# Modulation steps moved into the mixers' query and key stages, and a reordered beginning

## The chip, the cores and the metric
The kernel runs on one core of a Trainium2 chip. The metric is the device time of one execution in microseconds. Three runs of the kernel before gave 1868.36, 1869.28 and 1870.40 us, median 1869.28. The profile is of one further execution.

## The reference, cut to what matters
One inference step of a hybrid diffusion transformer, two layers, 384 tokens of width 1024 in three tiles of 128 (tile 0 context, tiles 1 and 2 latent). All is float32.
```
m = silu(c) @ w_ada + b_ada            # per layer and condition: 9 rows of 1024
x = layernorm(ALPHA*x + 0.5*m[2]*swiglu(modulate(x, m[0], m[1])))      # FFN 1
h = modulate(x, m[3], m[4])
u = h @ w_in                           # fourier | q latent | kv latent | rope key | na q,k,v
y_m = attention(rmsnorm(u_q) @ w_uq, [c_kv @ w_ukv | rope key], v)     # 8 heads
x = layernorm(ALPHA*x + m[5]*((g_f*y_f + g_m*y_m + g_n*y_n) @ w_out))  # gates: sigmoid(h @ w_gate)
x = layernorm(ALPHA*x + 0.5*m[8]*swiglu(modulate(x, m[6], m[7])))      # FFN 2
modulate(x, shift, scale) = ln(x)*(1+scale) + shift
```

## The kernel before
Matrices are multiplied as three products of rounded halves: a weight or activation is split into a high part (`whi`, cast on ACT, line 188) and the remainder (`wlo`, subtraction on DVE, line 193), and PE multiplies hi*hi, hi*lo and lo*hi. Nearly all other instructions carry line 77, where a helper issues them, so names of tiles tell them apart.

PSUM is one pool of eight banks (`psum`, tag "b") handed out in rotation: a new tile takes the bank of the one eight tiles earlier and waits until that one has been read. SBUF slots rotate likewise. SP issues the weight loads at places found by a planner (`make_plan`, `place`); elsewhere each engine's order comes from the scheduler that compiles the program, near program order. `begin` alone is under a manual schedule: there PE, ACT and DVE run in the order of the code.

The modulation rows of later sublayers are computed in pieces beside the main work. `ada_step` loads 128x1024 of `w_ada` and multiplies it into two accumulators `acc` on DVE (one per condition; the first step of a block is a TENSOR_SCALAR, the others SCALAR_TENSOR_TENSOR). After eight steps `ada_finish` transposes (`at`) and reduces (`red`) both on DVE, and three calls later `ada_place` puts a PE product `ada<-red,quad` into a bank, from which DVE adds the bias into `mod`. `ada_spend(n)` does n steps, up to a budget for each sublayer: 12 for the mixer of layer 0, 8 for that of layer 1. In the mixer it is called in `value` (nv), after `load_bias(0)` and before each nq and nk group.

`mixer_body` goes in this order: turns of the q latents (`qnT`), Fourier mixing (`fa`, `fo`, `oF`), the kv latents (`ckT`), `query` for three tiles (`q`, `qtok`), the rope key (`krT`), keys (`kn`, four groups, split by DVE into `k`), values (`v`, four groups, split into `vs`), turned queries (`qT`, split into `q`), then the Fourier branch `yb` in eight groups, copied by DVE to `mg`, and the attention, which begins with `s`. The mixer's head (uq, kv, uf; `qn` is the rms-normed q latent, `f` the split Fourier input) precedes it.

`begin` handles the first sublayer: 24 identity transposes (`warm`), statistics of the three tiles on DVE, normalised tiles `xn`, their transposes `xT`, copies `hf`, then for each of eight chunks the first modulation (`ada_first`: 16 small products `ada`, a DVE transpose `adas`; `ada_first_finish`: `adat`, `mod`), the modulated halves `hmh` and `hml`, and the first products `hd` of the FFN.
Of the kernel before, what the change touches and what calls it, by code (L numbers as in the profile page):

```python
# [8 lines left out]
F32 = mybir.dt.float32  # L9
F32R = mybir.dt.float32r  # L10
AF = mybir.ActivationFunctionType
ALU = mybir.AluOpType
AX = mybir.AxisListType
# [3 lines left out]
P = 128  # L17
# [71 lines left out]
class Kernel:  # L89
# [279 lines left out]
    def ada_setup(self):  # L369
        self.ada_blocks = [("g", (0, 0)), ("m", (0, 1), 0), ("m", (0, 1), 1), ("g", (0, 1)), ("m", (0, 2), 0), ("m", (0, 2), 1),  # L370
                           ("g", (0, 2)), ("m", (1, 0), 0), ("m", (1, 0), 1), ("g", (1, 0)), ("m", (1, 1), 0), ("m", (1, 1), 1),
                           ("g", (1, 1)), ("m", (1, 2), 0), ("m", (1, 2), 1), ("g", (1, 2))]
        self.ada_pos, self.ada_fin, self.ada_due = 0, [], []
        self.mod = {}
        self.gate_d = {}
        sel = self.fixed([P, 32], F32, "sel")
        self.nc.vector.tensor_reduce(out=sel, in_=self.ident.rearrange("p (q r) -> p r q", q=4), op=ALU.add, axis=AX.X)
        self.quad = self.fixed([P, 4, 32], F32, "quad")
        self.nc.gpsimd.tensor_copy(out=self.quad, in_=sel.unsqueeze(1).broadcast_to([P, 4, 32]))
        self.bad = [self.fixed([P, 72], F32, "bad") for _ in range(DEPTH)]  # L380

    def ada_bias(self, l):
# [240 lines left out]
    def transition(self, prev, nxt, mod):  # L623
# [65 lines left out]
            p()  # L689
        self.inhead = False  # L690

    def begin(self, nxt):
        nc = self.nc
        hf = [self.slot([P, 2, TOK], F32, "hf") for _ in range(4)]
        ns, mvs, rs = [], [], []

        def normal(t):
            n = self.slot([P, D], F32, "xn")
            if t == NT - 1:
                nc.vector.tensor_scalar(out=n, in0=self.x[t], scalar1=mvs[t][:, 0:1], scalar2=rs[t], op0=ALU.subtract, op1=ALU.mult)  # L700
            else:
                mr = self.small(1)
                nc.vector.scalar_tensor_tensor(out=mr, in0=mvs[t][:, 0:1], scalar=-1.0, in1=rs[t], op0=ALU.mult, op1=ALU.mult)
                nc.scalar.activation(out=n, in_=self.x[t], func=AF.Identity, scale=rs[t], bias=mr)
            ns.append(n)

        for t in range(NT):
            mvs.append(self.stats(self.x[t]))
            rs.append(self.rstd(mvs[t][:, 1:2], 1.0, 1e-6))
            if t:  # L710
                normal(t - 1)

        def turn(t, then=None, qs=range(2)):
            for q in qs:
                pt = self.psum("xT")
                for b in range(4):
                    dc = q * 4 + b
                    nc.tensor.transpose(pt[:, b * P:(b + 1) * P], ns[t][:, dc * P:(dc + 1) * P], self.ident)
                if then and q == 0:
                    then()  # L720
                for b in range(2):
                    o, i = hf[2 * q + b][:, :, t * P:(t + 1) * P], pt[:, b * 256:b * 256 + 256].rearrange("p (a b) -> p a b", a=2)
                    if b:
                        nc.scalar.copy(out=o, in_=i)
                    else:
                        nc.vector.tensor_copy(out=o, in_=i)

        piece = {0: 1, 1: 1, 2: 1, 3: 1, 4: 2, 6: 2}
        m = self.mod_tile((0, 0))

        hg = {}

        def shift(dc, *cds):
            h = hf[dc // 2][:, dc % 2]
            if dc not in hg:
                hg[dc] = self.slot([P, TOK], F32, "hg")
            g = hg[dc]
            for cd in cds:
                c = (slice(0, P), slice(P, TOK))[cd]
                sc, sh = m[:, 1, dc, cd:cd + 1], m[:, 0, dc, cd:cd + 1]  # L740
                nc.scalar.activation(out=self.hm[0][:, dc, c], in_=h[:, c], func=AF.Identity, scale=sc, bias=sh)
                nc.vector.tensor_scalar(out=g[:, c], in0=h[:, c], scalar1=sc, scalar2=sh, op0=ALU.mult, op1=ALU.add)
            for cd in cds:
                c = (slice(0, P), slice(P, TOK))[cd]
                nc.vector.tensor_tensor(out=self.hm[1][:, dc, c], in0=g[:, c], in1=self.hm[0][:, dc, c].bitcast(F32), op=ALU.subtract)

        turn(0)
        self.ada_bias(0)
        normal(NT - 1)
        self.held = []  # L750
        ahead = self.ada_first(0, 1)
        nxt.cold_unit(0)
        turn(1, self.high)
        self.ada_first_finish(0, 1, ahead)
        shift(0, 0)
        turn(2, qs=[0])
        shift(0, 1)
        self.low()
        turn(2, qs=[1])
        every = [(t, g) for t in range(NT) for g in range(HG)]  # L760
        for dc in range(KD):
            d1 = dc + 1
            if d1 < KD:
                nxt.cold_unit(d1)
            if dc:
                parts, i, j = [(p, t, g) for t, g in every for p in range(3)], 6, 9
            else:
                parts, i, j = [(p, t, g) for ps, ts in (((0, 1), (0,)), ((0, 1), (1, 2)), ((2,), range(NT))) for p in ps for t in ts for g in range(HG)], 12, 15
            if not dc:
                self.high()  # L770
                self.low()
            nxt.cold_head(dc, parts[:i])
            self.high()
            self.low()
            if d1 in piece:
                ahead = self.ada_first(d1, piece[d1])
            nxt.cold_head(dc, parts[i:j])
            if d1 in piece:
                self.ada_first_finish(d1, piece[d1], ahead)
            if d1 < KD:  # L780
                shift(d1, 0, 1)
            nxt.cold_head(dc, parts[j:])
            while self.held:
                self.high()
                self.low()
        self.held = None
        nxt.cold_finish()
        self.ada_bias(1)
        self.gate_start()
# [179 lines left out]
    def mixer_body(self, ph):  # L969
        nc, I, K, O, l = self.nc, self.I, self.K, self.O, ph.l  # L970
# [60 lines left out]
            ckT.append(kt)  # L1031

        def query(t):
            c = slice(t * P, (t + 1) * P)
            qk = self.slot([P, NH, HQ], F32, "qtok")
            for hh in range(2):
                b = self.psum("q")
                for kc in range(3):
                    w = self.W(("wuq", l, kc), "mla_w_uq", l, kc * P, 1, 0, 768)
                    self.mm3(b[:, 0:384], (qnT[kc][:, 0, c], qnT[kc][:, 1, c]),  # L1040
                             tuple(x[:, 0, hh * 384:hh * 384 + 384] for x in w), kc == 0, kc == 2)
                bv = b[:, 0:384].rearrange("p (h j) -> p h j", h=4)
                qs = qk[:, 4 * hh:4 * hh + 4]
                if t == 0:
                    nc.scalar.copy(out=qs, in_=bv)
                else:
                    nc.scalar.copy(out=qs[:, :, 0:64], in_=bv[:, :, 0:64])
                    self.rope(qs[:, :, 64:96], bv[:, :, 64:96], t - 1, 4)
            qtok.append(qk)
# [6 lines left out]
        pt = self.psum("krT")  # L1056
# [4 lines left out]
        k96 = [self.slot([HQ, 2, 512], F32R, "k96") for _ in range(NH)]  # L1061
        w = self.ukv(l, 0)
        for pr in range(4):
            b = self.psum("kn")
            for kc in range(2):
                lhs = tuple(x[:, kc, 2 * pr:2 * pr + 2].rearrange("p a b -> p (a b)") for x in w)
                self.mm3(b, lhs, (ckT[kc][:, 0], ckT[kc][:, 1]), kc == 0, kc == 1)
            for e in range(2):
                kk = k96[2 * pr + e]
                self.split(kk[0:64, 0], kk[0:64, 1], b[64 * e:64 * e + 64, :])  # L1070
                nc.vector.tensor_copy(out=kk[64:96], in_=krt[64:96].bitcast(F32))
        w = self.ukv(l, 1)
        vm = []
        for t in range(4):
            b = self.psum("v")
            for kc in range(2):
                self.mm3(b, (ckT[kc][:, 0, t * P:(t + 1) * P], ckT[kc][:, 1, t * P:(t + 1) * P]),
                         tuple(x[:, kc].rearrange("p a b -> p (a b)") for x in w), kc == 0, kc == 1)
            vm.append(self.split_v(b))
# [21 lines left out]
        for d in range(KD):  # L1101
            b = self.branch_chunk(l, 0, d, oF)
# [51 lines left out]
        for p2 in range(4):  # L1154
            for nme in ("nq", "nk"):
                self.ada_spend(1)
                b = self.psum(nme)
# [107 lines left out]
    def run(self):  # L1265
# [7 lines left out]
        self.mhalf = self.fixed([P, 1], F32, "mhalf")  # L1273
        nc.vector.memset(self.mhalf, -0.5)

        wp = self.psum("warm")
        for i in range(24):
            nc.tensor.transpose(wp[:, i % 4 * P:i % 4 * P + P], self.ident, self.ident)
        self.mask = self.fixed([P, 64], F32, "mask")
        self.rp = self.fixed([P, 2, 2, 32], F32, "rp")  # L1280
        self.ada_setup()
# [292 lines left out]
```

## Time and profile before
| | |
|---|---|
| runs | 1868.36 to 1870.40 us, median 1869.28 |
| profiled execution | 1866.74 us, span 1865.0 us |
| PE busy | 99% of the span |
| DVE busy | 1409.0 us, 76% |
| ACT busy | 785.3 us, 42% |
| DMA | mean 172 GB/s |

The span runs from the first to the last instruction. The profile marks an engine busy while it executes; a PE wait of a few microseconds is a hundredth of the span or less and can be seen only in the waits and in rows in order of time.

### The profile page before, as it was taken

To read this page: it belongs to the slowest core of one execution; us is meant where nothing else is said; L and a number is where in the kernel's file an instruction comes from. 1 tells how busy PE (TensorE), PEld (TensorE's weight loads), DVE (VectorE), ACT (ScalarE), POOL (GpSimd) and SP (SyncE) were. 2 spreads that over 40 slices of the span, in tenths; PEclk is the share of its full clock that TensorE was granted. 3 is DMA by queue.
4 is the path that set the end of the run, shared out by engine and by line. 5 is a ranking of instruction groups with operands and counts; after the bars stand their busy time and mean duration, and the time that the engine had idled before them with its cause. 6 is when DMAs were issued, how large, how long until landed. Compare 5 with 4: busy or idle time off the path is not lost. (4 is left out here: it accounts for less than half of the span.)

```text
span 1865.0 us, 27258 instructions
## 1 busy us (share of the span) xinstructions
PE 1842.9 (99%) x10568; PEld 1728.1 (93%) x10568; DVE 1409.0 (76%) x2206; ACT 785.3 (42%) x1305; POOL 94.7 (5%) x115
## 2 busy tenths in 40 slices
PE   8999999999999999999999999999999999999998
PEld 6899998999899999999999999989999998999997
DVE  6788888689997677888876888978798776533345
ACT  4433335556355453332453333355554553533330
POOL 0000002000100010000000000120001000000000
PEclk9999999999999999999999999999999999999999
DMA  9766656234835446666545666542356353444522
GB/s 325 264 224 212 206 209 207 88 102 126 234 109 188 125 148 221 196 226 219 188 159 186 221 220 219 193 157 89 113 177 183 104 190 130 133 135 125 145 92 79
DMA packets 225602, 320.22 MB, mean 172 GB/s; under 512 B 32784, under 2 KB 181888, under 8 KB 225344
## 3 DMA queue, kind: packets, MB, share of 16 engines
q1 hardware_dynamic: 223328, 313.88, 52.5%
q0 software_dynamic: 2112, 4.59, 0.6%
q8 instruction: 83, 1.36, 0.3%
q14 instruction: 47, 0.39, 0.1%
q10 hardware_dynamic: 32, 0.01, 0.0%
HBM read 312.32 MB, written 8.02 MB: 172 GB/s over the span
## 5 line engine op out<-in xcount | busy, mean ns | idle before, releaser
L193 DVE TENSOR_TENSOR wlo<-raw,whi 128x1024 fp32r<-128x1024 f32 (+4 forms) x420 | 488.7, 1181 | 148.7 <-ACT whi L188 68.0
L188 ACT CAST whi<-raw 128x1024 fp32r<-128x1024 f32 (+4 forms) x420 | 420.3, 1020 | 325.9 <-DVE wlo L193 83.7
L77 PE MATMUL w<-hmh,whi 128*128 128x384 f32 x1152 | 388.3, 337 | 0.8 <-ACT sl L77 0.8
L77 PE MATMUL w<-hmh,wlo 128*128 128x384 f32 x1152 | 387.1, 336 | 0.0
L77 PE MATMUL w<-hml,whi 128*128 128x384 f32 x1152 | 387.1, 336 | 0.0
L77 PE MATMUL y<-whi,sT 128*128 128x512 f32 x1050 | 335.1, 391 | 1.7 <-DVE sT L77 1.5
L77 DVE SCALAR_TENSOR_TENSOR acc<-raw,cs,acc 128x1024 f32<-128x1024 f32 x236 | 296.9, 1290 | 28.8 <-DMA raw<-in_w_ada_dram 28.5
L77 PEld LDWEIGHTS y<-whi,sT 128*128 128x128 f32 x1050 | 196.8, 188 | 41.1 <-DVE sT L77 2.1
L77 PEld LDWEIGHTS w<-hmh,whi 128*128 128x128 f32 x1152 | 216.6, 188 | 3.2 <-ACT sl L77 1.1
L77 PEld LDWEIGHTS w<-hml,whi 128*128 128x128 f32 x1152 | 216.6, 188 | 1.9
L77 PEld LDWEIGHTS w<-hmh,wlo 128*128 128x128 f32 x1152 | 216.6, 188 | 0.0
L77 PE MATMUL y<-wlo,sT 128*128 128x512 f32 x525 | 204.2, 389 | 0.0
L77 PE MATMUL g<-hmh,whi 128*128 128x384 f32 x384 | 132.5, 345 | 1.4 <-DVE qN L77 1.4
L77 PE MATMUL g<-hmh,wlo 128*128 128x384 f32 x384 | 129.8, 338 | 1.6 <-DVE wlo L193 1.6
L77 PE MATMUL g<-hml,whi 128*128 128x384 f32 x384 | 129.9, 338 | 0.0
L77 PEld LDWEIGHTS y<-wlo,sT 128*128 128x128 f32 x525 | 98.6, 188 | 18.1
L77 ACT CAST sT<-sl 128x384 fp32r<-128x384 f32 x72 | 37.1, 515 | 183.8 <-DVE sl L77 183.8
L77 PE MATMUL hd<-whi,hmh 128*128 128x256 f32 (+1 forms) x336 | 100.1, 300 | 1.6 <-ACT hmh L77 1.6
L77 PE MATMUL hd<-wlo,hmh 128*128 128x256 f32 (+1 forms) x336 | 99.0, 297 | 0.0
L77 PE MATMUL hd<-whi,hml 128*128 128x256 f32 (+1 forms) x336 | 98.9, 296 | 0.0
L77 ACT ACTIVATE sl<-w 128x384 f32<-128x384 f32 x72 | 35.4, 492 | 110.0 <-PE w L77 109.7
L77 POOL TENSOR_TENSOR st<-st,mhalf 128x1 f32<-128x1 f32 x48 | 43.9, 916 | 689.3 <-DVE st L77 689.2
(271 smaller groups left out, 2952.3 us busy)
## 6 DMA issues: line engine op xcount, KB each, us to landing
raw<-in_ffn_w_dram SPq DMA_DIRECT2D x244, 512.0 KB, 5.0
raw<-in_w_ada_dram SPq DMA_DIRECT2D x128, 512.0 KB, 4.9
raw<-in_w_gate_dram SPq DMA_DIRECT2D x48, 512.0 KB, 4.1
raw<-in_w_in_dram SPq DMA_DIRECT2D x32, 512.0 KB, 6.1
raw<-in_w_ada_dram SPq DMA_DIRECT2D x32, 256.0 KB, 5.9
raw<-in_w_out_dram SPq DMA_DIRECT2D x16, 512.0 KB, 6.8
raw<-gd SPq DMA_DIRECT2D x12, 512.0 KB, 5.1
raw<-in_ffn_w_dram SPq DMA_DIRECT2D x22, 256.0 KB, 5.8
```

Of the source, the lines that this page charges most:

```text
L77: r = f(*a, **kw)
L188: self.real.scalar.copy(out=hi, in_=r)
L193: self.real.vector.tensor_tensor(out=lo, in0=r, in1=hi.bitcast(F32), op=ALU.subtract)
```

## The change
Six edits: (1) the `sel` reduction and the `quad` copy move from the setup to behind the statistics; (2) 14 more identity transposes at the start of `begin`; (3) the tile before is normalised between the two halves of a tile's statistics; (4) turns and copies are separate, and the hf copies of tiles 1 and 2 come behind the first modulation; (5) `ada_first` comes ahead of the weight split of its turn; (6) the mixer spends modulation steps in `query` (1 each), before each kn group (1) and before v groups 1 and 3 (1), from the same budgets.
```
     def ada_setup(self):
...
-        sel = self.fixed([P, 32], F32, "sel")
-        self.nc.vector.tensor_reduce(out=sel, in_=self.ident.rearrange("p (q r) -> p r q", q=4), op=ALU.add, axis=AX.X)
-        self.nc.gpsimd.tensor_copy(out=self.quad, in_=sel.unsqueeze(1).broadcast_to([P, 4, 32]))
+        self.sel = self.fixed([P, 32], F32, "sel")
...
+    def warm(self, n):
+        wp = self.psum("warm")
+        for i in range(n):
+            self.nc.tensor.transpose(wp[:, i % 4 * P:i % 4 * P + P], self.ident, self.ident)
...
     def begin(self, nxt):
+        self.warm(14)
...
         for t in range(NT):
-            mvs.append(self.stats(self.x[t]))
+            st = self.small(12)
+            for h in range(2):
+                nc.vector.bn_stats(out=st[:, h * 6:h * 6 + 6], in_=self.x[t][:, h * 512:h * 512 + 512])
+                if t and h == 0:
+                    normal(t - 1)
+            mvs.append(self.moments(st, 2))
             rs.append(self.rstd(mvs[t][:, 1:2], 1.0, 1e-6))
-            if t:
-                normal(t - 1)
+        nc.vector.tensor_reduce(out=self.sel, in_=self.ident.rearrange("p (q r) -> p r q", q=4), op=ALU.add, axis=AX.X)
+        nc.gpsimd.tensor_copy(out=self.quad, in_=self.sel.unsqueeze(1).broadcast_to([P, 4, 32]))
...
-        turn(0)
+        for q in range(2):
+            copy(*turn(0, q))
...
-        turn(1, self.high)
+        wait = [turn(1, 0), turn(1, 1)]
+        self.high()
         self.ada_first_finish(0, 1, ahead)
         shift(0, 0)
-        turn(2, qs=[0])
+        wait.insert(1, turn(2, 0))
+        for _ in range(2):
+            copy(*wait.pop(0))
         shift(0, 1)
         self.low()
-        turn(2, qs=[1])
+        wait.append(turn(2, 1))
+        for w in wait:
+            copy(*w)
...
+            if d1 in piece:
+                ahead = self.ada_first(d1, piece[d1])
             self.high()
             self.low()
-            if d1 in piece:
-                ahead = self.ada_first(d1, piece[d1])
...
         def query(t):
+            self.ada_spend(1)
...
         for pr in range(4):
+            self.ada_spend(1)
             b = self.psum("kn")
...
         for t in range(4):
+            self.ada_spend(t % 2)
             b = self.psum("v")
```
On DVE, layer 0, before: the splits of the second to fourth kn group (`k`), a weight split among them.
```order
L77 TENSOR_TENSOR k_650_3491<-kn_3512,k_650_3491 64x512
L77 CAST k_650_3491<-krt_3486 32x1024
L77 CAST k_651_3492<-krt_3486 32x1024
L77 TENSOR_TENSOR k_651_3492<-kn_3512,k_651_3492 64x512
L193 TENSOR_TENSOR wlo_3530<-raw_3261,whi_3529 128x1024
L77 TENSOR_TENSOR k_652_3493<-kn_3525,k_652_3493 64x512
L77 CAST k_652_3493<-krt_3486 32x1024
L77 CAST k_653_3494<-krt_3486 32x1024
L77 TENSOR_TENSOR k_653_3494<-kn_3525,k_653_3494 64x512
L77 TENSOR_TENSOR k_654_3495<-kn_3542,k_654_3495 64x512
```
After, the same place: steps of modulation stand among the groups.
```order
L77 STREAM_TRANSPOSE at_3546<-acc_2399 128x1024
L77 STREAM_TRANSPOSE at_3549<-acc_2400 128x1024
L77 TENSOR_REDUCE red_3545<-at_3546 128x32
L77 TENSOR_REDUCE red_3545<-at_3549 128x32
L77 TENSOR_SCALAR acc_3552<-raw_3307,cs_156 128x1024
L77 TENSOR_SCALAR acc_3553<-raw_3307,cs_156 128x1024
L77 TENSOR_TENSOR k_657_3524<-kn_3558,k_657_3524 64x512
L77 CAST k_657_3524<-krt_3519 32x1024
L77 CAST k_658_3525<-krt_3519 32x1024
L77 TENSOR_TENSOR k_658_3525<-kn_3558,k_658_3525 64x512
L77 SCALAR_TENSOR_TENSOR acc_3552<-raw_3327,cs_156,acc_3552 128x1024
L77 SCALAR_TENSOR_TENSOR acc_3553<-raw_3327,cs_156,acc_3553 128x1024
```
The transposes, reductions and products of the modulation have come in between the k splits.

On PE, layer 0, before: the end of kn and the beginning of v.
```order
L77 MATMUL kn_3542<-ckT_3338,wlo_3311 128x512
L77 MATMUL kn_3542<-ckT_3348,whi_3310 128x512 x2
L77 MATMUL kn_3542<-ckT_3348,wlo_3311 128x512
L77 MATMUL v_3555<-whi_3397,ckT_3338 128x512
L77 MATMUL v_3555<-wlo_3398,ckT_3338 128x512
```
After, the same place.
```order
L77 MATMUL kn_3594<-ckT_3375,whi_3337 128x512 x2
L77 MATMUL kn_3594<-ckT_3375,wlo_3338 128x512
L77 MATMUL ada_3609<-red_3545,quad_104 128x64
L77 MATMUL v_3616<-whi_3430,ckT_3367 128x512
L77 MATMUL v_3616<-wlo_3431,ckT_3367 128x512
L77 MATMUL v_3616<-whi_3430,ckT_3367 128x512
```
The product of the modulation, which reads `red`, stands between kn and v.

On DVE in `begin`, before: statistics (`st`) of tiles 1 and 2, and among them the mean-and-scale products of tiles 0 and 1 (SCALAR_TENSOR_TENSOR).
```order
L77 BN_STATS st_180<-x_111 128x6 x2
L77 BN_AGGR st_183<-st_180 128x2
L77 TENSOR_SCALAR st_185<-st_183 128x1
L77 TENSOR_REDUCE sel_103<-ident_68 128x32
L77 SCALAR_TENSOR_TENSOR st_190<-st_174,st_178 128x1
L77 BN_STATS st_193<-x_113 128x6 x2
L77 BN_AGGR st_196<-st_193 128x2
L77 TENSOR_SCALAR st_198<-st_196 128x1
L77 SCALAR_TENSOR_TENSOR st_203<-st_183,st_187 128x1
```
After, the same place.
```order
L77 BN_STATS st_193<-x_109 128x6
L77 SCALAR_TENSOR_TENSOR st_196<-st_187,st_191 128x1
L77 BN_STATS st_193<-x_109 128x6
L77 BN_AGGR st_200<-st_193 128x2
L77 TENSOR_SCALAR st_202<-st_200 128x1
L77 BN_STATS st_206<-x_111 128x6
L77 SCALAR_TENSOR_TENSOR st_209<-st_200,st_204 128x1
L77 BN_STATS st_206<-x_111 128x6
L77 BN_AGGR st_213<-st_206 128x2
L77 TENSOR_SCALAR st_215<-st_213 128x1
L77 TENSOR_REDUCE sel_103<-ident_68 128x32
```
Each product stands behind the first half of the next tile's statistics, and the reduction into `sel` behind all of them.

## Rows read from the trace of the kernel before
**Rows 1.** Page, busy time by engine: us, share of the span, instructions.
```profile
PE 1842.9 (99%) x10568; PEld 1728.1 (93%) x10568; DVE 1409.0 (76%) x2206; ACT 785.3 (42%) x1305; POOL 94.7 (5%) x115
```

**Rows 2.** Waits of PE, by releaser: us in total, times, longest us.
```profile
PE xT L77 <- ACT xn L77: 2.8, 1, 2.8
...
PE g L77 <- DVE wlo L193: 1.6, 1, 1.6
...
PE g L77 <- DVE qN L77: 1.4, 1, 1.4
...
PE adat L77 <- DVE adas L77: 1.0, 1, 1.0
...
PE yb L77 <- DVE k L77: 0.8, 2, 0.4
```

**Rows 3.** Windows, qn product to split: us; PE, PEld, DVE, ACT, POOL; PEclk, DMA, GB/s.
```profile
340.40:379.90 39.50, 39.23 (x226) 35.47 (x224) 33.38 (x78) 22.86 (x44) 0.55 (x1) 1.00 0.30 95
...
1260.40:1303.00 42.60, 42.20 (x243) 38.47 (x242) 36.42 (x83) 25.94 (x49) 0.55 (x1) 1.00 0.27 88
```

**Rows 4.** Timeline of DVE, layer 0: start us, us, operation, count.
```profile
367.79 0.68 DVE L77 TENSOR_TENSOR k<-kn,k 64x512 fp32r<-64x512 f32 x1
...
379.22 0.69 DVE L77 TENSOR_TENSOR k<-kn,k 64x512 fp32r<-64x512 f32 x1
...
383.48 1.01 DVE L77 TENSOR_TENSOR q<-qT,q 96x384 fp32r<-96x384 f32 x2
```

**Rows 5.** Timeline of PE, layer 0, from v to s.
```profile
371.06 0.39 PE L77 MATMUL v<-whi,ckT 128*128 128x512 f32 x1
...
377.30 0.59 PE L77 MATMUL yb<-oF,whi 128*128 128x384 f32 x2
...
380.06 0.59 PE L77 MATMUL yb<-oF,whi 128*128 128x384 f32 x2 [0.43 <-DVE k L77]
...
394.72 1.50 PE L77 MATMUL s<-k,q 96*128 96x384 f32 x9
```

**Rows 6.** Timeline of DVE, a block's end and the next one's beginning, layer 0.
```profile
479.63 1.21 DVE L77 TENSOR_REDUCE red<-at 128x32 f32<-128x1024 f32 x1
...
480.76 1.24 DVE L77 STREAM_TRANSPOSE at<-acc 128x1024 f32<-128x1024 f32 x1
...
481.92 0.71 DVE L77 TENSOR_SCALAR acc<-raw,cs 128x1024 f32<-128x1024 f32 x1
...
482.55 1.21 DVE L77 TENSOR_REDUCE red<-at 128x32 f32<-128x1024 f32 x1
...
484.33 2.48 DVE L77 SCALAR_TENSOR_TENSOR acc<-raw,cs,acc 128x1024 f32<-128x1024 f32 x2
...
486.73 2.35 DVE L193 TENSOR_TENSOR wlo<-raw,whi 128x1024 fp32r<-128x1024 f32 x2
...
494.99 0.71 DVE L77 TENSOR_TENSOR mod<-ada,bad 32x16 f32<-32x16 f32 x4
```

**Rows 7.** Timeline of DVE, layer 1: v splits.
```profile
1301.72 1.88 DVE L77 TENSOR_TENSOR vs<-v,vs 128x512 fp32r<-128x512 f32 x3
```

**Rows 8.** Timeline of PE, layer 1: first s.
```profile
1314.73 1.50 PE L77 MATMUL s<-k,q 96*128 96x384 f32 x9
```

**Rows 9.** Window behind the two waits of g: columns as in Rows 3.
```profile
511.20:514.60 3.40, 3.40 (x13) 3.40 (x12) 3.40 (x5) 0.27 (x1) 1.28 (x1) 0.50 0.02 7
```

**Rows 10.** Timeline of DVE in begin: tile 1's statistics, tile 0's product.
```profile
6.09 1.28 DVE L77 BATCH_NORM_STATS2 st<-x 128x6 f32<-128x512 f32 x2
...
7.99 0.15 DVE L77 SCALAR_TENSOR_TENSOR st<-st,st 128x1 f32<-128x1 f32 x1
```

**Rows 11.** Timeline of PE in begin: the first tile's turns, the second's.
```profile
9.47 1.97 PE L77 MATMUL xT<-ident,xn 128*128 128x128 f32 x8 [2.84 <-ACT xn L77]
...
13.14 1.09 PE L77 MATMUL xT<-ident,xn 128*128 128x128 f32 x8
```

**Rows 12.** Tile warm: ns shortest, median, longest; first and last start us.
```profile
L77 PE MATMUL warm<-ident x24: 272/421/477, 1.4 to 6.2; 128*128 128x128 f32 x24
```

More of the change, by code (lines that the diff above doesn't have):

```diff
@@ L707, in begin, with turn, copy @@
         for t in range(NT):
-            mvs.append(self.stats(self.x[t]))
-            rs.append(self.rstd(mvs[t][:, 1:2], 1.0, 1e-6))
-            if t:
-                normal(t - 1)
[L713 to L726, printed above, removed]
+            st = self.small(12)
[4 more added lines that the diff above has]
+            mvs.append(self.moments(st, 2))
+            rs.append(self.rstd(mvs[t][:, 1:2], 1.0, 1e-6))
+        nc.vector.tensor_reduce(out=self.sel, in_=self.ident.rearrange("p (q r) -> p r q", q=4), op=ALU.add, axis=AX.X)
+        nc.gpsimd.tensor_copy(out=self.quad, in_=self.sel.unsqueeze(1).broadcast_to([P, 4, 32]))
+        def turn(t, q):
+            pt = self.psum("xT")
+            for b in range(4):
+                dc = q * 4 + b
+                nc.tensor.transpose(pt[:, b * P:(b + 1) * P], ns[t][:, dc * P:(dc + 1) * P], self.ident)
+            return t, q, pt
+        def copy(t, q, pt):
+            for b in range(2):
+                o, i = hf[2 * q + b][:, :, t * P:(t + 1) * P], pt[:, b * 256:b * 256 + 256].rearrange("p (a b) -> p a b", a=2)
+                if b:
+                    nc.scalar.copy(out=o, in_=i)
+                else:
+                    nc.vector.tensor_copy(out=o, in_=i)
         piece = {0: 1, 1: 1, 2: 1, 3: 1, 4: 2, 6: 2}
@@ L1274, in run @@
         nc.vector.memset(self.mhalf, -0.5)
-        wp = self.psum("warm")
-        for i in range(24):
-            nc.tensor.transpose(wp[:, i % 4 * P:i % 4 * P + P], self.ident, self.ident)
+        self.warm(24)
         self.mask = self.fixed([P, 64], F32, "mask")
```

## The prediction
> **What bounds the kernel now.** I read the busy line of the page first: PE is busy 1842.9 of 1865.0 us [rows 1]. All of PE's idle time is 22.1 us, so no change that leaves the matmuls as they are can win more than that and what the clock gives back, while any new wait of PE counts in full. The waits of PE come second [rows 2]: 2.8 us for the first normalised tile, 1.0 for the first transposed sums, 1.4 and 1.6 in a stretch of g products, and one small row that matters most here, yb waiting for DVE's k split, 0.8 us in two times, one in each mixer. Third come the windows of the two mixers [rows 3]: from the qn product to the last k split DVE is busy 33.38 of 39.50 us in layer 0, and in layer 1, to the third v split, 36.42 of 42.60. DVE has 6.1 and 6.2 us to spare there, with no modulation product in either stretch. Last I read the rows of DVE and PE in order of time. The k splits start at 367.79 and the last ends at 379.91 (379.22 + 0.69) [rows 4], although PE left the kn products for v at 371.06 [rows 5]; yb's second group, which wants the last k split's PSUM bank, started at 380.06 after waiting 0.43 [rows 5]. So DVE runs 9 us behind PE here, with no slack before the banks run out. Whatever is put on DVE ahead of the last k split, beyond its 6 us of idle time, delays yb.
>
> **The mixers.** Nine steps of modulation in layer 0 and eight in layer 1 move from the nv, nq and nk stages to query, kn and v. A step is one DMA and two DVE products over 128x1024. The moved steps complete a block in each mixer, so two transposes and two reductions come along, and in layer 0 two products that start a new block. Steps of starts in the rows of DVE give the prices [rows 6]: product 1.20 us (two from 484.33 to 486.73), transpose 1.16, reduction 1.13, starting product 0.63.
>
> Layer 0. By the order, twelve products, both transposes, both reductions and both starting products stand between the qn product and the last k split: four ahead of f, four more in front of the first k split or within it, four among the others. That is 12 x 1.20 + 2 x 1.16 + 2 x 1.13 + 2 x 0.63 = 20.2 us. Less the 6.1 us idle, the last k split ends 14.1 us later, at 394.0. On PE a further matmul, ada, now stands between kn and v and waits for the reductions; behind it are v, qT and yb, but it is released some 16 us ahead of the last k split, and v and qT took 6.2 us (371.06 to 377.30), so the bank remains the last wait. The ada bank shifts the rotation of eight by one: yb's first group now takes the bank of the last kn. It starts at 394.0 instead of 377.30, and the old wait of 0.43 goes: 16.7 - 0.4 = **+16.3 us**, seen where s starts (394.72 before [rows 5]).
>
> Layer 1. The order has sixteen products ahead of the second v split, and the transposes and reductions between the first two; no ada bank comes here. The fifth group of yb takes the bank of the third v, whose split ends at about 1303.0 (second of three from 1301.72 [rows 7]). Extra work ahead of it is 16 x 1.20 + 2 x 1.16 + 2 x 1.13 = 23.8 us, less 6.2 idle: 17.6, so 1320.6. Four of the eight groups remain, at (394.72 - 377.30 - 0.43) / 8 = 2.12 us each: s at 1329.1 instead of 1314.73 [rows 8], **+14.4 us**.
>
> What could cover this? Two bounds. From below: if no bank were waited for, PE would next need the q splits for s. Before, they end at 384.49 (383.48 + 1.01 [rows 4]), 10.2 us ahead of s. Layer 0 has then four more products (4.8) and four small mod additions (0.7 [rows 6]) ahead of them, 25.7 - 6.1 = 19.6, or +9.4; layer 1 by the same slack 17.6 - 10.2 = +7.4. From above: none of the 6 us idle is usable, as it lies in waits for ACT and POOL, and both numbers rise by up to 6; I do not believe that, since a late DVE finds those inputs ready. I take 16.3 and 14.4, because the 0.43 wait shows the bank deciding in each layer.
>
> **The clock after a stall.** Right behind the two waits of g, 1.4 and 1.6 us [rows 2], the granted clock was 0.50 of full, the lower level of 1.2 GHz, for 3.40 us [rows 9], which costs 1.7 us. PE will stand still for several microseconds in each mixer: one such stretch each while yb is on the path, **+3.4 us** (0 if it falls where DVE is the bound anyway, 6.8 with two each).
>
> **What is relieved.** From 479.63 on DVE runs reductions, transposes and products of a block without a gap [rows 6], is busy for all of the 3.40 us of [rows 9], and the two waits of g, 1.4 and 1.6, are for DVE [rows 2]. In layer 0 the steps go from there, so I take off both waits and the slow stretch behind them: 1.4 + 1.6 + 1.7 = **-4.7 us** (-3.0 if the clock still falls, -5.5 with small waits near by). In layer 1 no wait of PE shows in that stage: nothing.
>
> **The beginning.** The first tile's mean-and-scale product on DVE stood at 7.99 us behind both halves of the next tile's statistics, which began at 6.09, and the sel reduction; now it stands behind the first half alone [rows 10]. That is 1.1 us earlier for the normalised tile, and for the first xT, which waited 2.84 [rows 11]. The 14 turns cost nothing: PE was idle there. In before the eight xT took 1.97 us at the lower clock against 1.09 a little later [rows 11], so 0.9 if the clock holds. The ada products behind them come at the pace of weights that load in a saturated stretch, so not all of 2.0 reaches the first hd. Moving the transposed sums ahead of the weight split removes most of a 1.0 wait [rows 2], but hd's lo products then wait for that split, 1.2 us of DVE. I count **-1.3 us** for all of it (0 to -1.9, which is 1.1 + 0.9 and less).
>
> Whether identity turns hold the clock: in before the 24 turns shorten from 421 to 272 ns towards their end [rows 12], with nothing else on PE since the start, so there turns alone brought the clock up. The Trainium skill says the contrary ("TensorE: Matmul & The Clock Gate", Part 4: PE-mode transpose): transpose-mode matmuls don't engage the full clock. By that page the 14 turns would hold nothing, the beginning would give some 0.5 us rather than 1.3 (an estimate, with the 0.9 of the xT gone), and the sum below would be 28.9; the row of this trace speaks against it.
>
> The hf copies of tiles 1 and 2 go behind the first modulation; what that modulation gains their tiles' modulations lose, so nothing beside the 1.3. The moved loads meet DMA shares of 0.30 and 0.27 in the mixers' stretches [rows 3] and go out ahead by SP's own plan: nothing.
>
> **Sum.** 16.3 + 14.4 + 3.4 - 4.7 - 1.3 = +28.1 us. The profiled run took 1866.74 us in all for a span of 1865.0; it becomes 1894.8. The median of the three runs, 1869.28, lies 2.54 higher, so the forecast is 1897.4 us.
>
> **The rivals.**
> - *Banks do not decide, the q splits do* (chance 0.12): 9.4 + 7.4 + 0 to 3.4 for the clock - 6.0 (relief and beginning) = +10.8 to +14.2, so 1880.1 to 1883.5. For it: the wait on k is only 0.8 us in 1865 [rows 2]. Against it: that wait occurs in both layers at the same place, and PE has nothing between qT and yb to fall back on.
> - *The clock falls twice in each mixer and the beginning gives nothing* (0.08): 28.1 + 3.4 + 1.3 = +32.8, 1902.1. For it: PE stalls at ada and again at yb in layer 0, and at several groups of yb in layer 1. Against it: part of the slow time lies before a bank that is late anyway.
> - *Faster: DVE absorbs the moved products* (0.06). Its place is the stretch from qn to the last k split, its price what is left of 20.2 and 23.8 us above the idle time there, and it decides if that is under 3 us a layer. Then only -6.0 stands, 1863.3. For it: DVE is busy just 76% of the span [rows 1], and after s it is free again. Against it: the idle 6.1 us is a third of the added work, and the k splits stand behind it on the same engine.
>
> **How the numbers follow.** The forecast with its bounds has 0.72: mixers 30.7 +- 3, clock 0 to 6.8, relief -3 to -5.5, beginning 0 to -1.9, so 1890 to 1904. With the q-split rival the range goes from 1882 to 1905 us. About 0.2% (3.7 us) can be told from no change. 0.02 is left for cases not thought of. Slower 0.91 (the forecast and the first two rivals, less 0.01), same 0.03 (those two remainders), faster 0.06.
>
> **What would show it.** In the profile after: PE rows "yb" waiting for DVE k or vs with several microseconds each near 380 and 1300; ada waiting for red ahead of v in layer 0; the first s of each mixer 14 to 16 us later against the uf products; DVE full through both stretches; stretches of granted clock 0.50 in them; no wait of g for qN or wlo in layer 0; first xT about 1.1 us earlier, at the shorter spacing. It is wrong if yb starts right behind qT, or if the span grows by under 10 us.

## The result and the profile after
| | before | after |
|---|---|---|
| median of the timed runs | 1868.82 us (1866.82 to 1870.40, 4 runs) | 1891.63 us (1891.28 to 1894.08, 4 runs) |
| profiled span | 1865.0 us | 1892.3 us |

The changed kernel is slower: ratio 1.0125, 95% interval 1.0108 to 1.0143, or +22.8 us by the medians. The profiled pair lies 27.3 us apart: the profiled execution of before (1866.74 us) has a mean granted TensorE clock of 0.997 on record and that of after (1894.08 us) 0.990, while runs of before between 1871.3 and 1871.9 us have 0.994 and the run of after at 1891.28 us has 0.993, so part of the 27.3 goes with the clock (below).

PE's busy line on the page after, which answers to [rows 1]:
```profile
PE 1851.3 (98%) x10582; PEld 1734.5 (92%) x10582; DVE 1404.4 (74%) x2206; ACT 784.2 (41%) x1305; POOL 94.3 (5%) x115
```
And PE's waits after (us in total, times, longest), for [rows 2]:
```profile
PE yb L77 <- DVE k L77: 11.0, 3, 5.8
PE ada L77 <- DVE red L77: 6.2, 1, 6.2
PE qT L77 <- DVE k L77: 3.6, 2, 2.6
...
PE yb L77 <- DVE vs L77: 1.8, 1, 1.8
...
PE xT L77 <- ACT xn L77: 0.6, 1, 0.6
```
The small row yb for k has grown from 0.8 to 11.0 us, and ada, qT and yb for vs have joined it, with two smaller ones further up in the mixer, for late DVE work too (fa 1.3 and fo 0.6 us in all, half in each layer); the two waits of g are gone, and xT's 2.8 is 0.6.

The two mixers' windows on PE and DVE after, from the qn product to the same split as in [rows 3] (columns as there):
```profile
338.80:392.50 53.70, 39.86 (x216) 34.83 (x214) 52.84 (x96) 22.73 (x44) 1.46 (x1) 0.89 0.43 143
1271.90:1331.90 60.00, 49.75 (x261) 44.84 (x259) 59.09 (x102) 26.77 (x50) 1.46 (x1) 0.89 0.41 137
```
Layer 0's stretch takes 53.7 us instead of 39.5, layer 1's 60.0 instead of 42.6, and DVE is busy for all but 0.9 us of each. The 6 us of idle time were used up, and what was left over has lengthened the stretch.

DVE's timeline after, layer 0, with the last k split, which answers to [rows 4]:
```profile
391.86 0.69 DVE L77 TENSOR_TENSOR k<-kn,k 64x512 fp32r<-64x512 f32 x1
392.58 0.72 DVE L77 TENSOR_TENSOR mod<-ada,bad 32x16 f32<-32x16 f32 x4
```
And PE's timeline after, from ada to s, for [rows 5]:
```profile
377.19 0.66 PE L77 MATMUL ada<-red,quad 128*128 128x64 f32 x2 [6.17 <-DVE red L77]
...
387.55 0.85 PE L77 MATMUL qT<-ident,qtok 128*96 128x128 f32 x3 [2.60 <-DVE k L77]
392.69 0.98 PE L77 MATMUL yb<-oF,whi 128*128 128x384 f32 x2 [4.29 <-DVE k L77]
...
411.61 0.68 PE L77 MATMUL s<-k,q 96*128 96x384 f32 x3
```
yb starts 0.14 us behind the end of the last k split (391.86 + 0.69), that is, when the bank that this split reads comes free. The same of layer 1 after, with s of [rows 8]:
```profile
1317.14 0.98 PE L77 MATMUL yb<-oF,whi 128*128 128x384 f32 x2 [5.78 <-DVE k L77]
...
1322.29 0.98 PE L77 MATMUL yb<-oF,whi 128*128 128x384 f32 x2 [0.96 <-DVE k L77]
...
1332.23 0.62 PE L77 MATMUL yb<-oF,whi 128*128 128x384 f32 x2 [1.82 <-DVE vs L77]
...
1342.22 1.04 PE L77 MATMUL s<-k,q 96*128 96x384 f32 x5
```
There yb waits three times, and the last wait is for vs: the fifth group's bank.

The relief in layer 0 shows in s of the neighbourhood attention and the first pa behind it, in PE's timeline before:
```profile
505.57 1.62 PE L77 MATMUL s<-kN,qN 64*128 64x384 f32 x18
...
525.15 0.60 PE L77 MATMUL pa<-ident,pr 128*128 128x128 f32 x4
```
And after:
```profile
522.42 1.62 PE L77 MATMUL s<-kN,qN 64*128 64x384 f32 x18
...
537.06 0.60 PE L77 MATMUL pa<-ident,pr 128*128 128x128 f32 x4
```
s is 16.85 us later than before, pa 11.91: the stage between gives back 4.9 us. g no longer waits there (3.0 us before), and the granted clock is 1.00 from 522.4 to 537.1 us, where before it fell to 0.50 for 3.4 us [rows 9]. Another 1.0 us comes back before the output projection: its first product `wo` starts at 632.82 before and 643.72 after, 10.9 later. In the beginning, PE's timeline before has the second chunk's first hd here:
```profile
24.19 0.50 PE L77 MATMUL hd<-whi,hmh 128*128 128x512 f32 x1 [0.50 <-ACT hmh L77]
```
And after, with the first tile's turns beside [rows 11]:
```profile
8.29 1.09 PE L77 MATMUL xT<-ident,xn 128*128 128x128 f32 x8 [0.56 <-ACT xn L77]
...
22.39 0.50 PE L77 MATMUL hd<-whi,hmh 128*128 128x512 f32 x1 [0.97 <-ACT hmh L77]
```
xT begins 1.18 us earlier and takes 1.09 us, as at the full clock, instead of 1.97; the second chunk's hd is 1.8 us earlier.

### The profile page after: what moved, and what is told of

The parts are those of the page before. It is cut to its first block, busy times and chain, and to the rows that moved or that the text cites. A ratio compares the mean times of both kernels' runs of the same rounds, so it can differ in the third digit from the quotient of the medians.

```text
span 1892.3 us, 27275 instructions
## 1 busy us (share of the span) xinstructions
PE 1851.3 (98%) x10582; PEld 1734.5 (92%) x10582; DVE 1404.4 (74%) x2206; ACT 784.2 (41%) x1305; POOL 94.3 (5%) x115
```

## The experiments
All differences are between medians, against runs of the kernel before on the same chip. Theory D is the prediction's: DVE's added work delays the splits whose PSUM banks yb needs. Its rivals are theory B (the reordered beginning costs part of it), theory A (the modulation product on PE, which waits for the reductions, costs it) and theory Q (PE is late for the q splits, not for banks).

**The mixer's edit alone.** Edit, in the kernel before, at the places of the change:
```
+            self.ada_spend(1)
+            self.ada_spend(1)
+            self.ada_spend(t % 2)
```


> Before with the mixer's edit alone. Theory D (products on DVE ahead of the splits whose PSUM banks yb needs): the changed kernel's +22.8 us less what the beginning gave there (hd of the second chunk 1.8 us earlier): +24.6 us against before, between +21 and +29 (by the profiled spans +27.3 + 1.8). Theory B (part of the rise comes from the reordered beginning, through loads that meet later work): less than +20.


Measured: 1896.14 against 1868.99 us, ratio 1.0145 (1.0130 to 1.0160), +27.2 us. That is inside theory D's range and far from theory B's: the whole rise comes from this edit. It costs more alone than in the changed kernel, where the beginning takes some off.

**The beginning alone.** Edit, in the changed kernel:
```
-            self.ada_spend(1)
...
-            self.ada_spend(1)
...
-            self.ada_spend(t % 2)
```


> The changed kernel without the mixer's edit. Theory D: the second chunk's hd 1.8 us earlier stays to the end: -1.8 us against before, between -1 and -2.5, hd at 22.4 us in the trace. Theory B: no gain or a loss, 0 to +3. A clock that identity turns don't hold: -0.5.


Measured: 1866.08 us, 0.9983 (0.9973 to 0.9992), -2.9 us (-5.0 to -1.5). The reordered beginning is a gain; theory B falls. The gain is a little over the 1 to 2.5 expected. The profiled pair is 2.1 us apart, and these runs have a granted clock of 0.997 to 0.999 where before's have 0.994 to 0.997, so part of the 2.9 may go with the clock.

**Layer 1 alone.** Edit, in the changed kernel, for each of the three calls:
```
+            if l == 1:
+                self.ada_spend(1)
-            self.ada_spend(1)
```


> The changed kernel with the mixer's edit in layer 1 alone; layer 0 spends its steps where they were. Theory D: layer 1 costs 14.4 and 1.9 for the clock, the beginning gives 1.8: +14.5 us against before (12 to 17), so layer 0 has the other 8, its 18 less 5 in relief. Theory A (the modulation product on PE, which waits 6.2 us for the reductions ahead of v, is the main cost): there is none between kn and v in layer 1; its visible waits of PE are 9.6 us: +8 us at most. Theory Q (PE is late for the q splits, not for banks): 7.4 + 1.9 - 1.8 = +7.5 us.


Measured: 1879.84 us, 1.0065 (1.0047 to 1.0083), +10.9 us, under the expected 12 to 17, and about midway between theory D's 14.5 and theory Q's 7.5, so that the time alone does not tell them apart; the trace does. Against the beginning alone, layer 1 costs 13.7; layer 0, by difference from the changed kernel, 12.0. PE's waits and s in its timeline, layer 1:
```profile
1302.85 0.98 PE L77 MATMUL yb<-oF,whi 128*128 128x384 f32 x2 [5.77 <-DVE k L77]
...
1308.00 0.59 PE L77 MATMUL yb<-oF,whi 128*128 128x384 f32 x2 [1.24 <-DVE k L77]
...
1312.85 0.59 PE L77 MATMUL yb<-oF,whi 128*128 128x384 f32 x2 [0.41 <-DVE vs L77]
...
1317.95 0.58 PE L77 MATMUL yb<-oF,whi 128*128 128x384 f32 x2 [2.75 <-DVE vs L77]
...
1326.35 1.50 PE L77 MATMUL s<-k,q 96*128 96x384 f32 x9
```
With its beginning 2.9 us earlier (the offset just ahead of the mixer), the fifth group starts at 1320.85 on before's axis, where the prediction had 1320.6, and s at 1329.25 (1329.1). What was too large is the clock: here the last four groups run at the full clock, in the changed kernel they took 9.99 us instead of 8.40. The window of that stretch here (columns as in [rows 3]):
```profile
1310.00:1326.30 16.30, 13.14 (x75) 12.56 (x74) 15.98 (x21) 6.93 (x7) 0.00 (x0) 1.00 0.40 130
```
And in the changed kernel, the same four groups:
```profile
1332.00:1342.20 10.20, 9.96 (x48) 10.00 (x49) 8.37 (x14) 3.59 (x4) 0.00 (x0) 0.83 0.33 105
```
The granted clock is 1.00 in the one and 0.83 in the other. PE waits at yb, four times, and s follows yb without a wait: theory Q falls. A wait of PE for the reductions does not exist here, and the cost does: theory A does not explain layer 1.

**The casts on ACT.** Edit, in the changed kernel:
```
-                nc.vector.tensor_copy(out=kk[64:96], in_=krt[64:96].bitcast(F32))
+                nc.scalar.copy(out=kk[64:96], in_=krt[64:96].bitcast(F32))
```


> The changed kernel with the eight rope-key casts a layer (32x1024 into k, 0.65 us each) issued on ACT instead of DVE: the same result with 5.2 us less on DVE between the k splits. Theory D: the splits end 5.2 us earlier in each layer and yb with them: 22.8 - 10.4 = +12.4 us against before (+10 to +16, the upper end if ACT's casts become late themselves). Theory A: only the first group's casts (1.3 us) lie ahead of the reductions: +21. Were DVE's load not the cause: +22.8.


Measured: 1882.78 us, 1.0073 (1.0058 to 1.0088), +13.8 us: 9.0 less than the changed kernel. Taking 10.4 us of DVE work (16 casts of 0.65) out from between the splits returns 9 of them. In this run's trace layer 1's yb still waits for k (4.5 us) and vs (2.3), but layer 0's waits for DVE's `mod` additions (2.0 us) and no longer for a k split. So the run shows that DVE's load ahead of yb is what costs; that the bank is a k split's is shown for layer 0 by the changed kernel's rows and the next run.

**The modulation product on PE later.** Edit, in the changed kernel:
```
-        self.ada_due.append([3, lambda: self.ada_place(blk, red)])
+        self.ada_due.append([8 if blk == ("m", (0, 2), 0) else 3, lambda: self.ada_place(blk, red)])
```


> The changed kernel with one thing later: the modulation product on PE that stood between kn and v in layer 0 (it waited 6.2 us for the reductions) comes eight calls instead of three behind them, in the nv stage. All DVE work of the mixer's edit stays. Theory D: that wait was covered, since the last k split's bank comes free when it did (0.7 us sooner without the four mod additions behind it); without the ada bank yb's second group, not its first, wants it, so one group of yb (2.1 us) fits ahead: +22.8 - 2.1 = +20.7 us against before (+19 to +23). Theory A (that wait is the cost): 6.2 us less, +16.6.


Measured: 1890.96 us, 1.0115 (1.0100 to 1.0131), +22.0 us. PE's timeline, layer 0:
```profile
381.78 0.84 PE L77 MATMUL qT<-ident,qtok 128*96 128x128 f32 x3 [4.57 <-DVE k L77]
388.06 0.98 PE L77 MATMUL yb<-oF,whi 128*128 128x384 f32 x2 [5.43 <-DVE k L77]
...
393.20 0.98 PE L77 MATMUL yb<-oF,whi 128*128 128x384 f32 x2 [0.96 <-DVE k L77]
...
409.62 1.50 PE L77 MATMUL s<-k,q 96*128 96x384 f32 x9
```
The wait of 6.2 us for red is gone and has come back as 4.57 at qT and 5.43 at yb. The second group of yb waits until 393.20, and s comes 2.0 us earlier than in the changed kernel, as theory D had it (2.1); theory A, which had 16.6 in all, falls. By the medians only 0.8 of these 2.0 us are seen, less than their spread.

**Without the 14 turns.** Edit, in the beginning alone:
```
-        self.warm(14)
```


> The reordered beginning alone, without the 14 identity turns (the run with them gave -2.9 us against before). If turns hold the clock: the first eight xT at the lower clock, 1.97 instead of 1.09 us, and the ada products with them; 0.9 us or somewhat more lost: -2.0 (-1 to -2.5), first xT row at 0.21 us spacing. If turns don't hold it, as a page of the Trainium skill has it for transposes: the same xT as with them and -2.9.


Measured: 1866.75 us, 0.9988 (0.9979 to 0.9998), -2.2 us; the 0.7 to the run with turns lies within the intervals. The traces tell them apart. PE's timeline without the turns:
```profile
8.20 1.80 PE L77 MATMUL xT<-ident,xn 128*128 128x128 f32 x8 [2.07 <-ACT xn L77]
...
10.05 1.93 PE L77 MATMUL ada<-raw,cs 128*32 128x256 f32 x16
...
22.65 0.50 PE L77 MATMUL hd<-whi,hmh 128*128 128x512 f32 x1 [0.97 <-ACT hmh L77]
```
And with them, the beginning alone:
```profile
8.23 1.09 PE L77 MATMUL xT<-ident,xn 128*128 128x128 f32 x8 [0.33 <-ACT xn L77]
...
9.31 0.64 PE L77 MATMUL ada<-raw,cs 128*32 128x256 f32 x8
10.91 0.64 PE L77 MATMUL ada<-raw,cs 128*32 128x256 f32 x8 [0.95 <-DMA raw<-in_w_ada_dram]
...
22.32 0.50 PE L77 MATMUL hd<-whi,hmh 128*128 128x512 f32 x1 [0.96 <-ACT hmh L77]
```
Without turns the eight xT take 1.80 us, with them 1.09, and the granted clock from 8.2 to 9.4 us is 0.60 without and 1.00 with them: in this kernel identity turns hold the clock. The Trainium skill ("TensorE: Matmul & The Clock Gate", Part 4: PE-mode transpose), which the prediction weighed, has it that the full clock does not engage for transpose-mode matmuls; the measurement decides. But with the turns the ada products wait 0.95 us for their weights, and the second chunk's hd starts at 22.32 with them against 22.65 without: the turns are worth 0.3 us.

**Eight steps out of layer 0's mixer.** Edit, in the beginning alone, and again with the casts on ACT:
```
-        budget = {(0, 0): 36, (0, 1): 12, (0, 2): 36, (1, 0): 36, (1, 1): 8, (1, 2): 0}
+        budget = {(0, 0): 44, (0, 1): 4, (0, 2): 36, (1, 0): 36, (1, 1): 8, (1, 2): 0}
```


> The reordered beginning, mixer untouched, but the modulation budget moves 8 steps from the mixer of layer 0 into the first FFN (44 and 4 instead of 36 and 12), which empties the nq and nk stage as the mixer's edit did. Theory D with the relief as its own term: -2.9 and -4.9 (the drop seen between s and the next attention part): -7.8 us against before (-6 to -9). Rival: the first FFN's DVE, 83 to 91% busy, lets PE wait there: -2.9 plus up to 5.

> As the one with budgets 44 and 4, and the rope-key casts on ACT. Before had two waits of yb for k, 0.4 us each, and DVE was 9 us late there. Theory D: these two go, -0.8 more: -8.6 us against before (-7 to -10). If ACT becomes late with its own half of the splits: -7.8 or worse.


Measured: 1886.34 us, 1.0093 (1.0078 to 1.0107), +17.4 us, and 1890.82 us, 1.0117 (1.0103 to 1.0132), +21.8 us. Both expectations missed, for a reason of the edit: the first FFN calls for two steps 18 times, so 36 is all it spends, and the eight steps were done in a lump ahead of the output projection. DVE's timeline of the first:
```profile
629.31 16.83 DVE L77 SCALAR_TENSOR_TENSOR acc<-raw,cs,acc 128x1024 f32<-128x1024 f32 x14
646.05 2.37 DVE L77 STREAM_TRANSPOSE at<-acc 128x1024 f32<-128x1024 f32 x2
648.34 2.30 DVE L77 TENSOR_REDUCE red<-at 128x32 f32<-128x1024 f32 x2
```
And PE's:
```profile
650.79 0.66 PE L77 MATMUL ada<-red,quad 128*128 128x64 f32 x2 [25.30 <-DVE red L77]
```
PE stood still for 25.3 us. Ahead of that, the relief is there alone, in PE's timeline:
```profile
518.67 0.60 PE L77 MATMUL pa<-ident,pr 128*128 128x128 f32 x4
```
The first pa stands at 518.67 for 525.15 before, 6.5 us earlier, of which the beginning had given 1.5. The casts on ACT cost 4.5 us here: yb's waits for k rose from 0.9 to 5.2 us in all, and DVE's k splits of layer 0 now wait for ACT's part of k, five times, 1.0 to 1.8 us each. Where DVE isn't late, ACT becomes so.

**Eight steps in the first FFN, in fact.** Edit, in the beginning alone: the budgets as above, and in the FFN
```
-                    k.ada_spend(2)
+                    k.ada_spend(3 if (self.l, self.s) == (0, 0) and j % 2 == 0 and j >= 6 else 2)
```


> The reordered beginning, mixer untouched, 8 of layer 0's 12 mixer steps really spent in the first FFN (three a call in 8 of its 18 calls), not in a lump at the mixer's end as the budget alone left them. Theory D: DVE has 15% idle there and its splits are ahead of PE; relief alone: the chain before that lump stood 7.4 us earlier than before: -7.6 us against before (-6 to -9). Rival: DVE, 83 to 91% busy in the first FFN, makes PE wait for sT or wlo: up to +5 of it lost.


Measured: 1864.20 us, 0.9977 (0.9968 to 0.9987), -4.6 us: a miss of the expected 6 to 9. The rival was right that PE would wait there, though for sl and hmh, not for sT or wlo. Part of the relief went to new waits in that FFN and at the mixer's head (its waits of PE from 200 to 345 us, where before has 0.4 in all):
```profile
PE w L77 <- DVE sl L77: 2.1, 2, 1.5
PE w L77 <- ACT sl L77: 1.1, 1, 1.1
PE uq L77 <- ACT hmh L77: 1.0, 1, 1.0
```

**Query alone, layer 0 alone.** Edit, in the beginning alone:
```
         def query(t):
+            if l == 0:
+                self.ada_spend(1)
```


> The reordered beginning, and of the mixer's edit only the three steps in query, in layer 0 only. Six products, 7.2 us, ahead of the k splits, with 6.1 us of idle DVE time there, and 5 steps instead of 8 left in nq and nk. Theory D (only what exceeds the idle time delays yb): +1.1 in s, half to all of the relief of 4.9: -2.9 + 1.1 - 2.5 to -4.9 = -4.3 to -6.7 us against before; yb waits for k some 1.5 us in layer 0. If idle time could not be used: s +7.2, and +1 us in all.


Measured: 1863.32 us, 0.9973 (0.9962 to 0.9984), -5.5 us, as expected, and the lowest median of all. Its window from qn to the last k split, layer 0 (columns as in [rows 3]):
```profile
338.90:379.80 40.90, 39.67 (x226) 35.48 (x224) 39.94 (x84) 22.66 (x44) 1.46 (x1) 1.00 0.40 126
```
And PE's timeline, with yb's wait and s:
```profile
379.95 0.59 PE L77 MATMUL yb<-oF,whi 128*128 128x384 f32 x2 [0.41 <-DVE k L77]
...
394.59 1.50 PE L77 MATMUL s<-k,q 96*128 96x384 f32 x9
```
Of 7.2 us of products, some 5 went into idle time (6.1 before, 1.0 now); the stretch became 1.4 us longer and s came 1.4 later against a mixer that begins 1.5 earlier (394.59 + 1.48 - 394.72), where theory D had 1.1. yb's own wait is unchanged, 0.41 (1.5 was expected): PE had lost the time further up, at fa (0.66) and fo (0.31), to the same late DVE. A loss that was not forecast stands behind it: in the key stage nk waits 1.5 us for ACT's `whi` and 0.8 for DVE's `wlo`, which it does not before, and the stretch from nv to s of the neighbourhood attention is 2.8 us longer. The transposes and reductions that complete a block now fall on DVE from 461.57 us on, where before the first reduction came at 479.63 [rows 6]; that this is what made the weights late is not shown.

**Four steps in the gate pieces.** Edit, in the beginning alone, in `fill_f`:
```
+                if l == 0 and d < 4:
+                    self.ada_spend(1)
                 g = self.gate_chunk(l, 0, d)
```


> The reordered beginning, and four of layer 0's steps in the first four gate pieces of the latent attention, where DVE was idle 9 us of 45 and PE waited for nothing; 4 steps instead of 8 left in nq and nk. Theory D: 9.6 us of products fit or make DVE late without a wait; -2.9 - 2.5 to -4.9 = -5.4 to -7.8 us against before. If DVE's lag there meets the gate pieces' banks: up to +5.


Measured: 1868.32 us, 0.9995 (0.9986 to 1.0004), -0.5 us: a miss. A new wait stands in its list of PE's waits:
```profile
PE o L77 <- DVE ptl L77: 3.6, 1, 3.6
```
This wait, and the lower clock behind it (0.72 granted from 470 to 478 us), made the stretch from the first nv product to the first nq 6.9 us longer, and nk waits 1.5 us for `whi`; together they took the gain. DVE's timeline shows what came between: from 454.70 to 467.42 us stand the two transposes and two reductions that complete a block and the first products of the next, and the split ptl that PE waits for begins behind them at 467.35, where before it began at 461.37. Whether four steps without a block's end in them would fit was not tried.

## Why the prediction was right, point by point
- **The banks behind DVE** were the cause, as forecast, and sized well. From the qn product (338.77 in the trace after) to the end of the last k split (392.55) took 14.3 us longer; forecast 14.1. Counted from the mixer's beginning, layer 0's s came 18.5 us later, 16.6 without the 1.9 of the clock; forecast 16.3. Layer 1's came 16.1 us later, 14.5 without the 1.6 of the clock; forecast 14.4. In layer 1 the fifth group started within 0.3 us of the forecast, both in the changed kernel (11.4 us of delay ahead taken off) and in the run with layer 1 alone.
- **The idle time was usable**: 0.9 us of 6 were left. So the bound from above was no danger, and the q-split rival is refuted by the waits at yb in every run with the whole edit or layer 1's part of it.
- **The clock** was put at 3.4 us. In the profiled run it cost 1.9 in layer 0 (yb's eight groups took 18.9 instead of 17.0) and 1.5 to 1.6 in layer 1; in the run with layer 1 alone it cost nothing. It is a term with a spread of its own. The granted clocks on record (above) go with the 4.5 us between the profiled pair's 27.3 and the medians' 22.8: the pair sets one of before's shortest executions against the longest of after's four. The other runs have no trace, so in which stretches their clock fell stays open.
- **The relief**, forecast 4.7 with 5.5 at most, was 4.9 up to the first pa and 5.9 up to the output projection; the 4.9 were seen alone in the run with the steps in a lump.
- **The beginning**, forecast 1.3, gave 1.8 in the trace and 2.9 (1.5 to 5.0) by the medians. At the first hd 1.7 of the 2.0 us arrived. Behind it the prediction set hd's wait for the weight split (1.2 us) against the wait of 1.0 for the sums, and so put the gain too small: the wait for the sums went, none for the split came, and hd's waits for hmh grew by only 0.6 us.
- **A step it left out**: PE's wait at the second qT, 2.60 us, for a k split's bank, and those at fa and fo, 1.0 us. They lay ahead of the bank wait at yb and added nothing.

The forecast was 28.1 us, the profiled pair gives 27.3 and the medians 22.8. That the profiled pair comes so close is in part luck, since its two executions stand at opposite ends of their runs; the forecast of 1897.4 us carried the 2.54 by which before's median lay above its profile over to the changed kernel, whose median lies 2.5 below its profile. The range, too, was drawn narrower than its bounds: they add up to 1906.8 us at the upper end, not 1904. Where the 5.3 between forecast and medians lie is not shown term by term. By medians layer 1 cost 13.7 where 16.1 was forecast with the clock and 14.4 without, and layer 0 cost 12.0 where 13.3 and 11.6 were, so both sides fit with little of the clock's share and a relief somewhat larger; the beginning adds 1.6.

## What to carry to other kernels
Before moving work to an engine, add up that engine's idle time in the stretch it moves to: here 7.2 us against 6 of idle time cost 1.4, 20 and 24 cost what was over. Then look where the end of the moved work falls: a block's transposes and reductions went with the steps, and with four steps in the gate pieces they made PE wait 3.6 us in a stage that had been free of waits. A wait of 0.4 us on a releaser that is otherwise late by 9 is a sign that the slack is gone, and the longest new wait (6.2 us, for the reductions) can be one that costs nothing because a later one covers it.

## What was not expected of the hardware
A stall of the same length at the same place was followed by the lower clock in one run and not in another. In layer 1 of the mixer's edit alone the last stall of yb, and the window behind it (columns as in [rows 3]), are:
```profile
1334.05 0.59 PE L77 MATMUL yb<-oF,whi 128*128 128x384 f32 x2 [2.78 <-DVE vs L77]
...
1334.00:1344.00 10.00, 9.95 (x48) 9.98 (x49) 8.19 (x13) 3.28 (x3) 0.00 (x0) 0.83 0.34 107
```
The four groups took 9.99 us at a granted clock of 0.83. With layer 1 alone the stall was 2.75 us, behind three waits much like those here (5.77, 1.24 and 0.41 against 5.78, 1.51 and 0.45), and the four groups took 8.40 us at 1.00. Why is open. And ACT as a home for the 32x1024 casts gained 9.0 us where DVE was late and lost 4.5 where it wasn't.
